# Differential outputs kept in SBUF, later preparations, and quadrant sums from a whole copy of transposed h

## The chip, the core and the metric

The kernel runs on one core of one Trainium2 chip. The metric is the device time of one execution in microseconds (us), as the median of several runs. Beside it stands one profiled execution, from which every view of the trace comes.

## What is computed

Two layers of a decoder trunk over x of 1024 rows by 1024 channels in float32. Cut to what matters here:

```python
h = _rmsnorm(x, pre_g)
p = h @ w_in                       # q, k, v, gates, conv inputs, merge gates
y_fox  = _fox_attention(...)  * silu(fg)    # 8 heads of 64
o = _rmsnorm(a @ v, norm_g) * (1.0 - lam_init)   # differential attention, 4 heads of 128
y_diff = o * silu(dg)
y_conv = cb * _short_conv(cc * cx, conv_w) * silu(cg)
m = gates[0] * (y_fox @ w_fox) + gates[1] * (y_diff @ w_diff) + gates[2] * (y_conv @ w_conv)
x = x + _rmsnorm(m @ w_o, post_g)  # h of the next layer comes from this x
```

## The kernel before

**Numbers as pairs.** Every float32 operand of a matrix product is kept as two tiles, `hi` and `lo`: ScalarE (ACT) writes `hi`, a rounded copy, and VectorE (DVE) or GpSimd (POOL) writes `lo`, the rest (`split`, L373 and L374). One product is three matmuls (`mm3`, L352 to L354). Weights are loaded by SP into `wraw`, ACT makes `whi` (L277, L319) and POOL, or DVE, makes `wlo` (L280, L320).

**Head of a layer.** `norm_rows` normalises rows (`hn`, L402) and TensorE (PE) transposes them into PSUM tiles `T` of 128x512, of which there are two (L175). From each `T` come one `hi` and one `lo` piece of `ht`. So h stands transposed in 16 blocks: two halves of the rows, four pairs of channel groups, hi and lo. PE then runs a stretch of plain products of `ht` with the conv weights. Beside it `build_s` forms sums of h's quadrants (`s1` to `s4`, two sets j = 0 and 1) for Strassen products, seven in place of eight. A quadrant is hi plus lo, so the sum of two quadrants takes three adds on DVE (L445), and a set takes ten. Each sum is split into hi (ACT, L449) and lo (L451: DVE for s2 and s3, POOL for s1 and s4). The weights of the Strassen products need differences as well (`sw`, L322, on DVE) and are then split. DVE also runs the convolution (`cv`, L582 and L585) and gathers the products (`u` L564, `uv` L530).

**Tail of a layer.** Attention runs in eight windows, four fox, then four differential. A differential unit `g` of head `hd` ends in `squares` (ACT), a matmul with ones (PE, L1052), `norm` (ACT: Ln L1042, Exp L1043) and `out` (DVE, L1046), and ACT issues a DMA of the result to DRAM, `od` (L1048). `y_prep` for that head loads the whole head back, `o` (SP, L1098), and the gate `g` (SP, L1104), takes the sigmoid (ACT, L1114), multiplies (DVE, L1111) and splits the result into `y` (ACT L1116, POOL L1117). `merge_br` loads a weight `wraw<-wbr`, a merge gate `g<-mg` and `mf`, multiplies y by the weight (`T`, `F`, `S`, `O` are PSUM tiles) and gathers with L1143 and L1146. When the windows are over, PE has only these merges and the output projection.

**What sets the order.** Actions of `later(dt, fn)` are put on a heap with a due time on a model clock; the clock is moved by `tick` as main work is written, and `need(item)` runs the heap up to that item. The engines' orders are fixed when the program is built. An engine takes its instructions in that order; one that waits holds all behind it, and so does SP with its DMAs. `blk` tiles come from one pool of 41 blocks (`NBLK`) of 4 KB a partition; a tile for which no block is free waits for the last user of an old one.

Of the kernel before, what the change touches and what calls it, by code (L numbers as in the profile page):

```python
# [11 lines left out]
F32 = mybir.dt.float32  # L12
# [8 lines left out]
S = 1024  # L21
D = 1024
P = 128
# [112 lines left out]
class Trunk:  # L136
# [248 lines left out]
    def new_ht(self):  # L385
        return [[[self.blk([P, 2, 512], F32R, "ht") for _ in range(2)] for _ in range(4)] for _ in range(2)]

    def hk(self, h, k, o=0, n=512):

        return [t[:, k % 2, o:o + n] for t in self.hT[h][k // 2]]  # L390

    def norm_rows(self, xs, gB, hT, tb0, step):

        nc = self.nc
        ss = self.sm(4, "q")
        hs = [self.blk([P, D], F32, "hn") for _ in xs]
        for i0 in range(0, len(xs), step):
            for i in range(i0, i0 + step):
                nc.scalar.activation(hs[i], xs[i], AF.Square, accum_out=ss[:, i:i + 1])
            r = self.rstd(ss[:, i0:i0 + step], 1.0 / D)  # L400
            for i in range(i0, i0 + step):
                nc.vector.scalar_tensor_tensor(out=hs[i], in0=xs[i], scalar=r[:, i - i0:i - i0 + 1], in1=gB,  # L402
                                               op0=ALU.mult, op1=ALU.mult)
        for i in range(0, len(xs), 2):
            o = (tb0 + i) * P
            for kp in range(4):
                t = self.pT()
                for j in range(4):
                    k = 2 * kp + j // 2
                    self.transpose(t[:, j * P:(j + 1) * P], hs[i + j % 2][:, k * P:(k + 1) * P])  # L410
                hi, lo = (x[:, :, o:o + 256] for x in hT[kp])
                self.split(hi, lo, t.rearrange("p (k c) -> p k c", k=2))

# [21 lines left out]
    def build_s(self, L):  # L435
# [6 lines left out]
        for j in range(2):  # L442
            q = dict(a11=h0[j], a12=h0[j + 2], a21=h1[j], a22=h1[j + 2])
            f = {n: [t.rearrange("p k c -> p (k c)").bitcast(F32) for t in v] for n, v in q.items()}
            add = lambda o, a, b, op: nc.vector.tensor_tensor(out=o, in0=a, in1=b, op=op)  # L445
# [7 lines left out]

            g = {}
            for n, x, y, op in (("s1", "a21", "a22", ADD), ("s3", "a11", "a21", SUB)):
                t = g[n] = self.blk([P, 1024], F32, n)
                add(t, f[x][0], f[y][0], op)
                add(t, t, f[x][1], ADD)
                add(t, t, f[y][1], op)
                if n == "s1":  # L460
                    t2 = self.blk([P, 1024], F32, "s2")
                    add(t2, t, f["a11"][0], SUB)
                    add(t2, t2, f["a11"][1], SUB)
                    put("s2", t2)
                put(n, t)
            for x in range(2):
                nc.scalar.dma_start(L.a21[j, x], f["a21"][x])
            add(t2, f["a12"][0], t2, SUB)
            add(t2, t2, f["a12"][1], ADD)
            put("s4", t2)  # L470
            for n in ("a11", "a12", "a22"):
                L.a[n].append(q[n])

# [533 lines left out]
    def diff_unit(self, L, hd, g):  # L1007
# [14 lines left out]
        def stage2():  # L1022
# [10 lines left out]
            po = yield from self.pv_group(g, probs, vmm, W2D, 0.64)  # L1033
            t = self.tmp()
            o, r = t[:, :256], t[:, 256:512]

# [8 lines left out]
            def out():  # L1045
                nc.vector.scalar_tensor_tensor(out=o, in0=o, scalar=self.dgc[:, l:l + 1], in1=r,  # L1046
                                               op0=ALU.mult, op1=ALU.mult)
                nc.scalar.dma_start(L.o["d"][hd, :, g * 256:g * 256 + 256], o)  # L1048

# [3 lines left out]
            later(1.2, norm)  # L1053
            later(2.0, out)

# [38 lines left out]
    def y_prep(self, L, kind, c):  # L1094

        nc, later = self.nc, self.clock.later
        o, g = self.blk([P, S], F32, "o"), self.blk([P, S], F32, "g")
        nc.sync.dma_start(o, L.o[kind][c])  # L1098
        if kind == "f":
            rb = self.blk([P, S], F32, "rb")  # L1100
# [6 lines left out]
        for h in range(2):  # L1107
            o1, g1, hi, lo = (t[:, h * 512:h * 512 + 512] for t in (o, g, *y[:2]))
            if kind == "f":
                nc.gpsimd.tensor_tensor(out=o1, in0=o1, in1=rb[:, h * 512:h * 512 + 512], op=ALU.mult)  # L1110
            mul = lambda o1=o1, g1=g1: nc.vector.tensor_tensor(out=o1, in0=o1, in1=g1, op=ALU.mult)  # L1111
            later(0.0, mul)
            if raw:
                later(0.0, lambda g1=g1: nc.scalar.activation(g1, g1, AF.Sigmoid))  # L1114
                later(0.6, mul)
            later(1.0, lambda o1=o1, hi=hi: nc.scalar.copy(hi, o1))  # L1116
            y.append(later(1.6, lambda o1=o1, hi=hi, lo=lo: nc.gpsimd.tensor_tensor(  # L1117
                out=lo, in0=o1, in1=hi.bitcast(F32), op=ALU.subtract)))
# [82 lines left out]
    def layer(self, l):  # L1201
# [10 lines left out]
        L.g = {"fg": dt([4, P, S], "fg"), "dg": dt([4, P, S], "dg"), "mg": dt([16, P, S], "mg")}  # L1212
        L.o = {"f": dt([4, P, S], "of"), "d": dt([4, P, S], "od")}
        L.ff = self.smalls.tile([P, 8, 8], F32, tag="ff", name=self.nm("ff"), bufs=1)
# [21 lines left out]
        for pair in rest:  # L1236
            self.gates_spilled(L, *pair)
        self.run_behind()
        self.reload_a21(L)
        run(self.v_unit(L, "f", 1, self.bank))  # L1240
# [166 lines left out]
```

## Time and profile before

| | |
|---|---|
| median of three runs | 2555.74 us (2550.59 to 2557.41) |
| the profiled execution | 2551.78 us, of which the span in the trace is 2550.0 us |
| TensorE clock granted, mean | 0.983 of full |
| PE busy | 2424.3 us, 95% of the span |
| DVE, ACT, POOL busy | 1551.5, 1113.6, 807.2 us |
| chain that ended last | PE 75%, DVE 10%, POOL 4%, ACT 4%, issue 4%, DMA 3% |

[...] The four stretches that follow are the head and the tail of the two layers: about 20 to 125 us and 1270 to 1395 us, and about 1050 to 1140 us and 2317 to 2405 us.

### The profile page before, as it was taken

How to read it: one execution, taken by the hardware profiler on the slowest of the kernel's cores; microseconds unless marked ns; L12 is line 12 of the kernel's file. 1: busy time of each engine (PE TensorE's matmuls, PEld its weight loads, DVE VectorE, ACT ScalarE, POOL GpSimd, SP SyncE). 2: the span in 40 equal slices, each digit the busy share in tenths (PEclk: the TensorE clock that was granted, in tenths of full speed). 3: DMA queues.
4: the chain of work that ended last, by engine and by line, in shares of the span. 5: the costliest groups of instructions: out<-in, count | busy, mean ns of one | idle time of the engine just before them, and what ended most of it. 6: DMA issues, size and time to landing. Idle time of an engine off the chain costs nothing.

```text
span 2550.0 us, 35609 instructions
## 1 busy us (share of the span) xinstructions
PE 2424.3 (95%) x13112; PEld 2045.7 (80%) x13112; DVE 1551.5 (61%) x2809; ACT 1113.6 (44%) x2264; POOL 807.2 (32%) x565
## 2 busy tenths in 40 slices
PE   7899999999999999979997999999999999999898
PEld 6677887788889788758976778887889897887688
DVE  6966465645665665646578664356465646656554
ACT  4224333335565555454432242233365645445543
POOL 1566334431111112451035662355211111124500
PEclk9899999999999999989998999999999999999899
DMA  4012224542223335634521122344422223355434
GB/s 168 33 50 98 91 93 141 165 146 59 70 75 97 115 102 159 213 146 141 187 103 42 50 91 86 101 145 136 159 75 60 68 93 109 110 170 192 182 108 182
DMA packets 123709, 293.95 MB, mean 115 GB/s; under 512 B 16256, under 2 KB 41216, under 8 KB 123536
## 3 DMA queue, kind: packets, MB, share of 16 engines
q1 hardware_dynamic: 68720, 216.89, 24.8%
q10 hardware_dynamic: 54816, 74.79, 9.6%
q8 instruction: 104, 1.70, 0.3%
q14 instruction: 69, 0.57, 0.1%
HBM read 200.26 MB, written 72.48 MB: 107 GB/s over the span
## 4 chain that ended last, share of the span: by engine, by line
PE 75%; DVE 10%; POOL 4%; ACT 4%; issue 4%; DMA 3%; ACTq 0%; SPq 0%; POOLq 0%; DVEq 0%
PE F L352 11%; PE F L354 10%; PE F L353 10%; PE S L352 5%; PE S L354 5%; PE S L353 5%; PE T L175 4%; PE T L352 3%; PE T L354 3%; PE T L353 3%; PE S L836 3%; PE S L837 2%; DVE s L445 2%; POOL wlo L320 2%; PE O L354 2%
## 5 line engine op out<-in xcount | busy, mean ns | idle before, releaser
L280 POOL TENSOR_TENSOR wlo<-wraw,whi 128x1024 fp32r<-128x1024 f32 (+2 forms) x93 | 194.3, 2093 | 875.6 <-ACT whi L277 761.4
L352 PE MATMUL F<-ht,wlo 128*128 128x512 f32 x792 | 331.0, 418 | 0.0
L354 PE MATMUL F<-ht,whi 128*128 128x512 f32 x792 | 315.9, 399 | 0.0
L353 PE MATMUL F<-ht,whi 128*128 128x512 f32 x792 | 313.7, 396 | 0.0
L320 POOL TENSOR_TENSOR wlo<-sw,whi 128x512 fp32r<-128x512 f32 x160 | 229.0, 1442 | 216.3 <-ACT whi L319 190.6
L320 POOL TENSOR_TENSOR wlo<-wraw,whi 128x1024 fp32r<-128x1024 f32 x80 | 160.4, 2007 | 168.3 <-ACT whi L319 158.7
L319 ACT CAST whi<-sw 128x512 fp32r<-128x512 f32 x160 | 96.0, 619 | 246.1 <-DVE sw L322 106.5
L354 PEld LDWEIGHTS F<-ht,whi 128*128 128x128 f32 x792 | 149.5, 189 | 32.4
L875 DVE TENSOR_TENSOR pt<-T,pt 128x512 fp32r<-128x512 f32 (+1 forms) x240 | 147.9, 633 | 43.6 <-ACT pt L874 41.1
L352 PEld LDWEIGHTS F<-ht,wlo 128*128 128x128 f32 x792 | 151.0, 191 | 24.4 <-ACT ht L373 0.4
L353 PEld LDWEIGHTS F<-ht,whi 128*128 128x128 f32 x792 | 150.7, 190 | 24.0
L988 ACT ACTIVATE p<-S,sm 128x512 f32<-128x512 f32 (+2 forms) x192 | 110.5, 580 | 132.7 <-DVE sm L984 61.4
L277 ACT CAST whi<-wraw 128x1024 fp32r<-128x1024 f32 (+2 forms) x126 | 117.8, 939 | 91.6 <-PE F L354 26.9
L982 DVE TENSOR_REDUCE sm<-S 128x1 f32<-128x512 f32 (+2 forms) x192 | 103.0, 553 | 79.5 <-PE S L840 50.6
L874 ACT CAST pt<-T 128x512 fp32r<-128x512 f32 (+1 forms) x240 | 124.5, 544 | 57.5 <-PE T L175 37.8
L836 PE MATMUL S<-qk,qk 128*128 128x512 f32 (+2 forms) x384 | 138.8, 361 | 6.5 <-ACT p L988 6.3
L175 PE MATMUL T<-ident,p 128*128 128x128 f32 x864 | 128.8, 274 | 2.0 <-DVE pt L875 0.9
L837 PE MATMUL S<-qk,sw 128*128 128x512 f32 (+2 forms) x384 | 129.3, 342 | 0.0
L908 ACT ACTIVATE p<-p,sm 128x384 f32<-128x384 f32 (+7 forms) x128 | 99.5, 777 | 62.6 <-DVE sm L901 54.3
L319 ACT CAST whi<-wraw 128x1024 fp32r<-128x1024 f32 x80 | 66.7, 834 | 137.6 <-PE S L354 40.6
L352 PE MATMUL F<-whi,ht 128*128 128x256 f32 (+1 forms) x416 | 122.8, 295 | 0.0
L354 PE MATMUL F<-whi,ht 128*128 128x256 f32 (+1 forms) x416 | 117.5, 282 | 0.0
(376 smaller groups left out, 6993.8 us busy)
## 6 DMA issues: line engine op xcount, KB each, us to landing
wraw<-wt SPq DMA_DIRECT2D x128, 512.0 KB
mg<-tmp ACTq DMA_DIRECT2D x64, 256.0 KB
sw<-qk ACTq DMA_DIRECT2D x256, 64.0 KB
g<-mg SPq DMA_DIRECT2D x32, 512.0 KB
wraw<-wo SPq DMA_DIRECT2D x32, 512.0 KB
x<-x SPq DMA_DIRECT2D x24, 512.0 KB
wraw<-wbr SPq DMA_DIRECT2D x48, 256.0 KB
m<-tmp ACTq DMA_DIRECT2D x32, 256.0 KB
```

Of the source, the lines that this page charges most:

```text
L175: self.nc.tensor.transpose(out, x, self.ident)
L277: nc.scalar.copy(hi, raw)
L280: getattr(nc, eng).tensor_tensor(out=lo, in0=raw, in1=hi.bitcast(F32), op=ALU.subtract)
L319: nc.scalar.copy(w[0][:, o], f)
L320: nc.gpsimd.tensor_tensor(out=w[1][:, o], in0=f, in1=w[0][:, o].bitcast(F32), op=ALU.subtract)
L352: nc.tensor.matmul(ps, wl, xh, start=start and i == 0, stop=False)
L353: nc.tensor.matmul(ps, wh, xl, start=False, stop=False)
L354: nc.tensor.matmul(ps, wh, xh, start=False, stop=stop and i == n - 1)
L836: nc.tensor.matmul(ps[:, :wp], q[:, i * P:(i + 1) * P], k[:, c0:c0 + wp], start=True, stop=False)
L837: nc.tensor.matmul(ps[:, :wp], qsw[:, (i % 2) * P:(i % 2) * P + P], k[:, c0:c0 + wp], start=False, stop=not last)
L874: self.clock.later(0.1, lambda: nc.scalar.copy(hi, T[:, n0:]))
L875: done = self.clock.later(0.6, lambda: nc.vector.tensor_tensor(out=lo, in0=T[:, n0:], in1=hi.bitcast(F32), op=ALU.subtract))
```

## The change

Three parts.

**A whole copy of transposed h.** `new_ht` makes three tiles for each place: hi, lo, and a float32 tile with the whole value. `norm_rows` fills the third with a copy on ACT from the same PSUM tile `T`. `build_s` reads only the third, so one add makes a sum of two quadrants. A layer has 16 such copies (128x512) more and its L445 adds go from 20 to 8. The 24 blocks are held until the gates are through; then `self.hT` keeps hi and lo alone.

**Differential outputs in SBUF.** A head's output gets a block `od` at its first unit; the units write into it, and `y_prep` waits for the last one (`od_done`) and works in it. The DMAs of L1048 (16 a layer, 128 KB) and the loads of L1098 for these heads (4 a layer, 512 KB) are gone.

**Later due times.** In `y_prep` the steps move from 0.0, 0.0, 0.6, 1.0, 1.6 to 4.0, 4.0, 4.6, 5.0, 5.6, and the fox heads' multiplication on POOL, until now at once, is asked for at 3.0.

```diff
     def new_ht(self):
-        return [[[self.blk([P, 2, 512], F32R, "ht") for _ in range(2)] for _ in range(4)] for _ in range(2)]
+        return [[[self.blk([P, 2, 512], dt, "ht") for dt in (F32R, F32R, F32)] for _ in range(4)] for _ in range(2)]
...
-                hi, lo = (x[:, :, o:o + 256] for x in hT[kp])
-                self.split(hi, lo, t.rearrange("p (k c) -> p k c", k=2))
+                hi, lo, f = (x[:, :, o:o + 256] for x in hT[kp])
+                tv = t.rearrange("p (k c) -> p k c", k=2)
+                self.split(hi, lo, tv)
+                nc.scalar.copy(f, tv)
...
-            f = {n: [t.rearrange("p k c -> p (k c)").bitcast(F32) for t in v] for n, v in q.items()}
+            f = {n: v[2].rearrange("p k c -> p (k c)") for n, v in q.items()}
...
-            for n, x, y, op in (("s1", "a21", "a22", ADD), ("s3", "a11", "a21", SUB)):
-                t = g[n] = self.blk([P, 1024], F32, n)
-                add(t, f[x][0], f[y][0], op)
-                add(t, t, f[x][1], ADD)
-                add(t, t, f[y][1], op)
...
-            add(t2, f["a12"][0], t2, SUB)
-            add(t2, t2, f["a12"][1], ADD)
+            t1, t2, t3 = (self.blk([P, 1024], F32, n) for n in ("s1", "s2", "s3"))
+            add(t1, f["a21"], f["a22"], ADD)
+            add(t2, t1, f["a11"], SUB)
+            put("s2", t2)
+            put("s1", t1)
+            add(t3, f["a11"], f["a21"], SUB)
+            put("s3", t3)
...
+            add(t2, f["a12"], t2, SUB)
             put("s4", t2)
...
-            t = self.tmp()
-            o, r = t[:, :256], t[:, 256:512]
+            r = self.tmp((P, 256))
+            if g == G_ORDER[0]:
+                L.od[hd] = self.blk([P, S], F32, "od")
+            o = L.od[hd][:, g * 256:g * 256 + 256]
...
-                nc.scalar.dma_start(L.o["d"][hd, :, g * 256:g * 256 + 256], o)
...
-            later(2.0, out)
+            end = later(2.0, out)
+            if g == G_ORDER[-1]:
+                L.od_done[hd] = end
...
-        nc.sync.dma_start(o, L.o[kind][c])
-        if kind == "f":
+        if kind == "d":
+            while c not in L.od_done:
+                yield 0.0
+            self.clock.need(L.od_done[c])
+            o = L.od[c]
+        else:
+            o = self.blk([P, S], F32, "o")
+            nc.sync.dma_start(o, L.o[kind][c])
...
-            later(0.0, mul)
+            later(4.0, mul)
...
-            later(1.0, lambda o1=o1, hi=hi: nc.scalar.copy(hi, o1))
-            y.append(later(1.6, lambda o1=o1, hi=hi, lo=lo: nc.gpsimd.tensor_tensor(
+            later(5.0, lambda o1=o1, hi=hi: nc.scalar.copy(hi, o1))
+            y.append(later(5.6, lambda o1=o1, hi=hi, lo=lo: nc.gpsimd.tensor_tensor(
```

The change moves instructions at three places. Line numbers of the kernel after are two to six lines off those of before: L414 is the new copy, L447 the add (L445 before), L453 the lo (L451), L451 the hi (L449), L578 and L581 the convolution (L582, L585), L560 the gathering (L564), L1109 the load of the gate (L1104).

DVE in the head of the second layer, second set of sums, before. `s3_2082` is the last sum that takes three adds, `sw` of the row with a single `wraw` is the weight difference of the product with s3:

```order
L451 TENSOR_TENSOR s_2079_12126<-s_2077_12122,s_2078_12125 128x1024
L445 TENSOR_TENSOR s_2082_12133<-ht_10686,ht_10694 128x1024
L445 TENSOR_TENSOR s_2077_12122<-ht_10690,s_2077_12122 128x1024
L445 TENSOR_TENSOR s_2082_12133<-s_2082_12133,ht_10687 128x1024
L445 TENSOR_TENSOR s_2077_12122<-s_2077_12122,ht_10691 128x1024
L322 TENSOR_TENSOR sw_11920<-wraw_11901 128x512
L445 TENSOR_TENSOR s_2082_12133<-s_2082_12133,ht_10695 128x1024
L564 TENSOR_TENSOR u_11885<-u_11885,O_12175 128x512
```

The same place after (`s_2094` is s3, `sw_11934` the difference, `u_11899<-u_11899,O_12177` the gathering of the last plain product):

```order
L447 TENSOR_TENSOR s_2094_12128<-ht_10680,ht_10692 128x1024
L447 TENSOR_TENSOR s_2093_12127<-ht_10686,s_2093_12127 128x1024
L560 TENSOR_TENSOR u_11898<-u_11898,S_12075 128x512
L453 TENSOR_TENSOR s_2100_12141<-s_2094_12128,s_2099_12140 128x1024
L322 TENSOR_TENSOR sw_11923<-wraw_11914,sw_11923 128x512
L578 TENSOR_SCALAR cv_11900<-u_11898,par 128x1024
L581 SCALAR_TENSOR_TENSOR cv_11900<-u_11898,par,cv_11900 128x1023
L581 SCALAR_TENSOR_TENSOR cv_11900<-u_11898,par,cv_11900 128x1022
L560 TENSOR_TENSOR u_11899<-u_11899,T_12151 128x512
L560 TENSOR_TENSOR u_11899<-u_11899,O_12177 128x512
L578 TENSOR_SCALAR cv_11901<-u_11899,par 128x1024
L322 TENSOR_TENSOR sw_11934<-wraw_11915 128x512
```

Four adds stood ahead of the difference and one behind it; now all sums are done before the plain products end, and one step of the convolution stands right ahead of the difference.

ACT in the same head, the last four tiles `T`, before (`a<-ht` are DMAs of a quadrant to DRAM):

```order
L373 CAST ht_10692<-T_11844 128x2x256
L467 DMA a_11883<-ht_10692 128x1024
L373 CAST ht_10694<-T_11851 128x2x256
L373 CAST ht_10696<-T_11858 128x2x256
L467 DMA a_11883<-ht_10693 128x1024
L373 CAST ht_10698<-T_11865 128x2x256
```

And after, where each copy L414 waits for the lo (DVE) of the same tile, and the transposes of the next tile but one wait for the copy:

```order
L373 CAST ht_10687<-T_11855 128x2x256
L464 DMA a_11897<-ht_10687 128x1024
L414 COPY ht_10689<-T_11855 128x2x256
L373 CAST ht_10690<-T_11863 128x2x256
L464 DMA a_11897<-ht_10688 128x1024
L414 COPY ht_10692<-T_11863 128x2x256
L373 CAST ht_10693<-T_11871 128x2x256
L464 DMA a_11897<-ht_10690 128x1024
L414 COPY ht_10695<-T_11871 128x2x256
L373 CAST ht_10696<-T_11879 128x2x256
```

A copy now stands between one tile's hi and the next tile's.

SP in the tail of the first layer, the last two heads, before:

```order
L1098 DMA o_10165<-od_328 128x1024
L1104 DMA g_10166<-dg_325 128x1024
L1098 DMA o_10183<-od_328 128x1024
L1104 DMA g_10184<-dg_325 128x1024
L272 DMA wraw_10189<-wbr 128x512
L1128 DMA g_10195<-mg_326 128x1024
L1131 DMA mf_10197<-m_321 128x1024
```

And after:

```order
L1109 DMA g_10160<-dg_349 128x1024
L1109 DMA g_10176<-dg_349 128x1024
L272 DMA wraw_10180<-wbr 128x512
L1134 DMA g_10186<-mg_350 128x1024
L1137 DMA mf_10188<-m_345 128x1024
```

The load of the last head's output, which waited for the write of that output, no longer stands ahead of the gate and the weight.

## Rows read from the trace of the kernel before

**Rows 1.** PE's waits, 60 to 125 us: line, waited for, us in total, times, longest

```profile
PE S L352 <- ACT s L449: 5.1, 1, 5.1
PE F L352 <- ACT s L449: 4.1, 1, 4.1
...
PE F L353 <- DVE s L451: 1.2, 1, 1.2
```

**Rows 2.** PE's waits, 1300 to 1400 us

```profile
PE F L352 <- POOL wlo L320: 8.6, 1, 8.6
PE T L175 <- DVE hn L402: 4.4, 2, 2.8
PE T L352 <- POOL wlo L320: 4.0, 1, 4.0
PE S L352 <- POOL wlo L320: 1.0, 1, 1.0
```

**Rows 3.** PE's waits, 1085 to 1140 us

```profile
PE T L352 <- POOL wlo L280: 8.2, 1, 8.2
PE O L1029 <- ACT pt L874: 7.2, 2, 4.9
```

**Rows 4.** PE's waits, 2350 to 2405 us

```profile
PE F L352 <- POOL wlo L280: 9.2, 1, 9.2
PE O L1029 <- ACT pt L874: 2.7, 2, 2.3
PE S L352 <- POOL wlo L280: 1.7, 1, 1.7
```

**Rows 5.** Ten windows at half clock: us, busy (instructions) of PE, PEld, DVE, ACT, POOL, PEclk, DMA

```profile
1130.70:1137.60 6.90, 3.52 (x8) 2.82 (x9) 6.03 (x8) 4.36 (x8) 4.84 (x4) 0.51 1.03 408
...
1352.60:1362.80 10.20, 4.03 (x10) 3.17 (x11) 10.20 (x8) 3.62 (x5) 5.68 (x4) 0.50 0.00 1
...
sum 58.04, PE 37.50 PEld 30.15 DVE 44.59 ACT 23.46 POOL 33.17; mean PE 3.75 PEld 3.02 DVE 4.46 ACT 2.35 POOL 3.32
```

**Rows 6.** Lines L445, L373, L374 by form: ns min/median/max, first and last start

```profile
L445 DVE TENSOR_TENSOR s<-s,ht x28: 1209/1224/3424, 47.6 to 1356.4; 128x1024 f32<-128x1024 f32 x28
L445 DVE TENSOR_TENSOR s<-ht,ht x8: 1211/3423/3428, 41.9 to 1346.9; 128x1024 f32<-128x1024 f32 x8
...
L373 ACT CAST ht<-T x32: 578/587/602, 13.6 to 1311.0; 128x512 fp32r<-128x512 f32 x32
...
L374 DVE TENSOR_TENSOR ht<-T,ht x32: 675/691/693, 16.3 to 1311.6; 128x512 fp32r<-128x512 f32 x32
```

**Rows 7.** The chain of waits that ended last, 1340 to 1360 us, by line

```profile
by line: DVE s L445 63.0%; DVE sw L322 12.2%; DVE s L451 11.8%; issue 7.4%; ACT s L449 5.3%; DVE u L564 3.0%; DVEq L451 0.1%
```

**Rows 8.** Timeline, 1354 to 1360 us: start us, us, engine, line, instruction

```profile
1352.44 3.41 DVE L445 TENSOR_TENSOR s<-s,ht 128x1024 f32<-128x1024 f32 x2
1355.78 0.68 DVE L322 TENSOR_TENSOR sw<-wraw 128x512 f32<-128x512 f32 x1
...
1357.18 1.54 POOL L320 TENSOR_TENSOR wlo<-sw,whi 128x512 fp32r<-128x512 f32 x1 [3.55 <-ACT whi L319]
```

**Rows 9.** Timeline of SP, ACT and POOL, 1122 to 1134 us

```profile
1124.95 0.32 SPq L1098 DMA_DIRECT2D o<-od  x1
...
1123.15 0.33 ACTq L1048 DMA_DIRECT2D od<-tmp  x1
1130.26 1.28 ACT L1114 ACT_TABLE_LOAD   x1 [6.62 <-DMA g<-dg]
...
1132.76 1.26 POOL L280 TENSOR_TENSOR wlo<-wraw,whi 128x512 fp32r<-128x512 f32 x1 [6.98 <-ACT whi L277]
```

**Rows 10.** Timeline of ACT, 1095.5 to 1102.5 us

```profile
1095.92 1.28 ACT L1114 ACT_TABLE_LOAD   x1
...
1101.58 0.96 ACT L874 CAST pt<-T 128x512 fp32r<-128x512 f32 x2
```

**Rows 11.** Timeline of DVE, 1299 to 1306.5 us

```profile
1300.23 4.57 DVE L402 SCALAR_TENSOR_TENSOR hn<-x,y,gB 128x1024 f32<-128x1024 f32 x2
```

More of the change, by code (lines that the diff above doesn't have):

```diff
@@ L385, in new_ht @@
     def new_ht(self):
-        return [[[self.blk([P, 2, 512], F32R, "ht") for _ in range(2)] for _ in range(4)] for _ in range(2)]
+        return [[[self.blk([P, 2, 512], dt, "ht") for dt in (F32R, F32R, F32)] for _ in range(4)] for _ in range(2)]
     def hk(self, h, k, o=0, n=512):
-        return [t[:, k % 2, o:o + n] for t in self.hT[h][k // 2]]
+        return [t[:, k % 2, o:o + n] for t in self.hT[h][k // 2][:2]]
     def norm_rows(self, xs, gB, hT, tb0, step):
@@ L452, in put @@
                 L.a[n].append([t.rearrange("p (k c) -> p k c", k=2) for t in (hi, lo)])
-            g = {}
-            for n, x, y, op in (("s1", "a21", "a22", ADD), ("s3", "a11", "a21", SUB)):
-                t = g[n] = self.blk([P, 1024], F32, n)
-                add(t, f[x][0], f[y][0], op)
-                add(t, t, f[x][1], ADD)
-                add(t, t, f[y][1], op)
[L460 to L467, printed above, removed]
-            add(t2, f["a12"][0], t2, SUB)
-            add(t2, t2, f["a12"][1], ADD)
+            t1, t2, t3 = (self.blk([P, 1024], F32, n) for n in ("s1", "s2", "s3"))
[5 more added lines that the diff above has]
+            put("s3", t3)
+            for x, t in enumerate(q["a21"][:2]):
+                nc.scalar.dma_start(L.a21[j, x], t.rearrange("p k c -> p (k c)").bitcast(F32))
+            add(t2, f["a12"], t2, SUB)
             put("s4", t2)
             for n in ("a11", "a12", "a22"):
-                L.a[n].append(q[n])
+                L.a[n].append(q[n][:2])
     def reload_a21(self, L):
@@ L1096, in y_prep @@
         nc, later = self.nc, self.clock.later
-        o, g = self.blk([P, S], F32, "o"), self.blk([P, S], F32, "g")
-        nc.sync.dma_start(o, L.o[kind][c])
-        if kind == "f":
+        g = self.blk([P, S], F32, "g")
+        if kind == "d":
[6 more added lines that the diff above has]
+            nc.sync.dma_start(o, L.o[kind][c])
             rb = self.blk([P, S], F32, "rb")
@@ L1109, in y_prep @@
             if kind == "f":
-                nc.gpsimd.tensor_tensor(out=o1, in0=o1, in1=rb[:, h * 512:h * 512 + 512], op=ALU.mult)
+                later(3.0, lambda o1=o1, rb1=rb[:, h * 512:h * 512 + 512]: nc.gpsimd.tensor_tensor(
+                    out=o1, in0=o1, in1=rb1, op=ALU.mult))
             mul = lambda o1=o1, g1=g1: nc.vector.tensor_tensor(out=o1, in0=o1, in1=g1, op=ALU.mult)
-            later(0.0, mul)
+            later(4.0, mul)
             if raw:
-                later(0.0, lambda g1=g1: nc.scalar.activation(g1, g1, AF.Sigmoid))
-                later(0.6, mul)
-            later(1.0, lambda o1=o1, hi=hi: nc.scalar.copy(hi, o1))
-            y.append(later(1.6, lambda o1=o1, hi=hi, lo=lo: nc.gpsimd.tensor_tensor(
+                later(4.0, lambda g1=g1: nc.scalar.activation(g1, g1, AF.Sigmoid))
+                later(4.6, mul)
+            later(5.0, lambda o1=o1, hi=hi: nc.scalar.copy(hi, o1))
+            y.append(later(5.6, lambda o1=o1, hi=hi, lo=lo: nc.gpsimd.tensor_tensor(
                 out=lo, in0=o1, in1=hi.bitcast(F32), op=ALU.subtract)))
@@ L1212, in layer @@
         L.g = {"fg": dt([4, P, S], "fg"), "dg": dt([4, P, S], "dg"), "mg": dt([16, P, S], "mg")}
-        L.o = {"f": dt([4, P, S], "of"), "d": dt([4, P, S], "od")}
+        L.o = {"f": dt([4, P, S], "of")}
+        L.od, L.od_done = {}, {}
         L.ff = self.smalls.tile([P, 8, 8], F32, tag="ff", name=self.nm("ff"), bufs=1)
@@ L1238, in layer @@
         self.run_behind()
+        self.hT = [[t[:2] for t in half] for half in self.hT]
         self.reload_a21(L)
```

## The prediction

> **What bounds the kernel now.** I read the shares of busy time first: PE is busy for 95% of the span, so a gain has to come from the other 5% and from matmuls that run at the half clock. Then I read PE's waits, stretch by stretch. They gather in two places of each layer: the head, where the quadrant sums are made, and the tail, where attention has ended and the merges go on. In the first head PE waits for the sums themselves, 5.1 + 4.1 + 1.2 = 10.4 us [rows 1]. In the second head it waits 8.6 + 4.0 + 1.0 = 13.6 us for the low part of a weight [rows 2], but that is only the last link. The chain of waits over that stretch puts 63% on L445, the adds [rows 7], and the timeline says why: the difference `sw` that the weight is made of starts at 1355.78 us, behind adds of 3.41 us for two, and POOL's lo starts at 1357.18 and lasts 1.54 [rows 8]. So DVE bounds that stretch, not POOL. In the tails PE waits 8.2 and 7.2 us in the first layer [rows 3], and 9.2 + 2.7 + 1.7 = 13.6 us in the second [rows 4]. The 8.2 us end on the lo of a weight at 1132.76; before it ACT waited 6.62 us for the gate `g<-dg` [rows 9]. SP could ask for that gate only after `o<-od` at 1124.95, and that load waited for the write `od<-tmp` of 1123.15, so SP's line was shut by one transfer and opened too late for everything behind it [rows 9]. The 7.2 us wait for `pt` of ACT, which from 1095.92 did a table load and the steps of `y_prep` and reached the `pt` casts at 1101.58 [rows 10].
>
> After a wait the clock is at half: the granted clock reads 0.50 in ten stretches at these places, and PE worked 37.50 us in them [rows 5]. At most half of that, 18.75 us, is lost.
>
> **Part 1, adds away, copies added.** A layer loses 12 of 20 adds. One add took 1.22 us in the median where both inputs are sums or pieces, and 3.42 where two pieces of h are read [rows 6], so 12 x 1.22 = 15 to 12 x 3.42 = 41 us of DVE time. What of it counts is the wait that it caused, the 10.4 and the 13.6 us. Against it stands the copy on ACT. It is not in the trace; the nearest row is the hi of the same tile, 0.587 us [rows 6]. In the order of ACT it stands behind the tile's lo of 0.691 [rows 6], and the transposes of the next tile but one wait for it. A turn of a tile is then 0.59 + 0.69 + 0.59 = 1.87 us, and since ACT takes hi, copy, hi, copy, four tiles of a row pair need 4 x 1.87 = 7.5 us. Before, they needed between 4 x 0.59 + 0.69 = 3.1 and 4 x 1.28 = 5.1. So a row pair takes 2.4 to 4.4 us more; I take 3.4.
>
> Nothing in the trace shows ACT and DVE reading one PSUM tile together, so the turn of 1.87 rests on the order alone. [...]
>
> *First head.* All rows of x are there at the start, so little stands between the tiles: between one row pair's 3.4 and two pairs' 6.8 us I take 6, late for the plain products. With 12 adds fewer, s2 and s3 are ready before PE asks, so the 10.4 us go. Next late is the weight of the product with s3: its difference stands on DVE behind three steps of the convolution. The nearest rows for one such step are the 128x1024 adds, 1.2 to 3.4 us [rows 6], so 3.7 to 10 us, of which the products ahead hide about half: 4.5, with ends 0 and 8. Sum: -10.4 + 6 + 4.5 = +0.1; ends -7 and +6.
>
> *Second head.* Here the rows come from the output projection two at a time. The norm of the last pair (two `hn`, 4.57 us from 1300.23 [rows 11]) stands on DVE behind the third pair's lo pieces and so starts 3.4 later; with the last pair's own 3.4 that is up to 6.8. But PE's order now has whole products of the first half between these transposes, and the 4.4 us that PE waits for `hn` today [rows 2] stay about what they are; I take 2.5 as seen by PE, ends 0 and 6.8. The 13.6 us go: all sums are done before the plain products end, one step of the convolution (1.2 to 3.4) stands ahead of the difference, and three Strassen products ahead of its user. I leave 2.5 for what is late next, POOL's lo pieces in line, ends 0 and 6. Sum: -13.6 + 2.5 + 2.5 = -8.6; ends -13.6 and -0.8.
>
> **Parts 2 and 3, the tails.** They take away 16 writes a layer, 0.33 us of ACT each [rows 9], and four loads on SP. SP's line then holds, for the last head, the gate, the weight and the merge inputs, and none waits for the last unit's output any more: the gate waits only for a block that the first head's y frees. From SP's opening at 1124.95 to the gate's landing it took 5.3 us [rows 9], and this now passes beside attention. PE ran out of work at 1134.0 - 8.2 = 1125.8. Next late is ACT: after the last unit's norm, which is done by 1123.15 when its write is issued [rows 9], come the sigmoid's table of 1.28, some four activations and casts of 0.6 and the weight's hi among them, then POOL's 1.26: 1123.15 + 1.28 + 4 x 0.6 + 1.26 = 1128.1. It comes somewhat earlier since fewer table loads stand between the last norms, and somewhat later by waits on DVE between the steps: 1127 to 1129. So 2.5 of the 8.2 us stay in the first layer and 3 of the 9.2 in the second; ends 0 and 6. The waits for `pt` lie elsewhere: the steps of `y_prep` are asked for 4 us later, so ACT's order has the `pt` casts ahead of them and a merge product stands ahead of PE's last matmuls with `pt`. But the same sigmoid table load stays among the exponentials, so I keep half: 3.6 of 7.2, and 2.2 of 4.4. Sums: -(8.2 + 7.2) + 2.5 + 3.6 = -9.3, ends -15 and -3; and -13.6 + 3 + 2.2 = -8.4, ends -13 and -3.
>
> **Blocks.** The copies hold 8 more blocks of 41 in the head, the outputs up to 4 in the windows. I cost that at nothing, since the waits for blocks that I see in the order end on work that lies well back. If that cover is gone, one load comes late and costs what the gate cost, 5.3 us.
>
> **Clock.** Where a wait goes, its half-clock stretch goes with it. Of the 18.75 us I take back 10.5, about in the share of the waits that go; ends 3 and 16.
>
> **The sum.** 0.1 - 8.6 - 9.3 - 8.4 - 10.5 = -36.7 us against the profiled run of 2551.8: 2515.1. The median of the runs lies 4.0 above the profiled one; with the same distance the forecast is 2519 us.
>
> **Rivals.** *Only one place pays.* If the copies eat the heads' gain, the tails alone give 17.7 and half the clock, 5, so 2533 us; if ACT's table loads hold the tails as the gate did, the heads alone give 8.5 and 5, so 2542. For it speaks that ACT is in order and has to do both norm and sigmoid at the end; against it that the wait on the gate is 6.62 us of idle ACT, which is room.
>
> *Nothing to be measured.* Both happen: the heads give the copies what the adds gave up, and the tails save 3 each: 2549 to 2556. For it speaks that PE's two transposition tiles are the narrow point in the first head; against it that the chain over the second head is 63% adds.
>
> *Slower.* The copies in line with the tiles are seen in full: four row pairs a layer, two layers, 8 x 3.4 = 27 us, while the weights' low parts on POOL hold the products as before, so the heads give nothing; less the tails' 17.7 it is 2565 us. It decides if PE has no other work beside the transposes, in both heads. In the first pairs of a row half PE does have it, which speaks against. [...]
>
> *It doesn't do what it says.* The order shows the adds, writes and loads gone, so I give this nothing.
>
> **How the numbers follow.** The forecast (2503 to 2532) has 0.64, one place 0.22 (2532 to 2546), no change 0.08, slower 0.06. The range: the five terms have half-widths of 5 to 7 us, some 13 together if they are independent, so 2519 - 16 = 2503 below; above it takes in the rival of one place, 2546. What is left out is no change and slower, 0.14. About 0.3%, 8 us, can be told from no change, so faster is 0.64 + 0.22 = 0.86, same 0.08, slower 0.06.
>
> **What would show it.** In the head: L447 eight times a layer; PE's waits for ACT and DVE sums in the first head gone; the wait for L320 in the second under 3 us; against it longer waits of transposes for the copy and for `hn`. In the tail: SP asks for the last gate before 1115 us, the wait for L280 falls to 1 to 4 us, `pt` to about half. Fewer than ten half-clock stretches. The prediction is wrong if plain products end more than 7 us later than before in both heads, or if the tail's wait is back at 8 us under another name.

## The result and the profile after

The changed kernel takes 2523.82 us (median; 2521.85 to 2525.12), the kernel before, run beside it, 2556.39 (2550.59 to 2557.41). The ratio is 0.9877 with an interval of 0.9859 to 0.9894: faster by 32.6 us, where 2519 us (36.7 less) had been forecast, with a range of 2503 to 2546. The profiled execution of after took 2525.12 us, 1.3 above its median, whereas that of before lay 4.6 below its own; so the two spans are only 26.8 us apart.

The head of the page of after; PE had been busy 2424.3 us of a span of 2550.0:

```profile
span 2523.2 us, 35542 instructions
...
PE 2416.4 (96%) x13112; PEld 2040.0 (81%) x13112; DVE 1536.6 (61%) x2785; ACT 1126.8 (45%) x2294; POOL 809.5 (32%) x565
```

PE does the same 13112 matmuls. Its busy time fell by 7.9 us, which goes with the clock (below), and its idle time from 125.7 to 106.8, by 18.9. To see where, I cut each profiled execution at four points that all kernels have: the first matmul of attention (L704 before, L700 after) and the first of the output projection, in each layer. Lengths of the pieces in us, worked out from the start times of these matmuls; the last three columns anticipate the experiments below:

| piece | before | after | forecast of the difference, clock included | measured | copy first | third `sw` buffer | both |
|---|---|---|---|---|---|---|---|
| to first attention (first head) | 570.1 | 570.7 | -2.9 | +0.6 | 559.0 | 563.8 | 555.2 |
| attention and first tail | 615.8 | 603.2 | -11.5 | -12.6 | 603.6 | 602.9 | 600.7 |
| output projection, second head | 649.4 | 641.0 | -12.2 | -8.4 | 637.4 | 631.2 | 628.8 |
| attention and second tail | 613.8 | 607.5 | -10.1 | -6.3 | 605.4 | 603.6 | 602.7 |
| last output projection | 100.9 | 100.9 | 0 | 0 | 100.8 | 100.8 | 100.8 |

(The forecast is the prediction's four sums with the 10.5 us of the clock spread over them, 3.0, 2.2, 3.6 and 1.7 in the order of the table; this split is mine, the prediction gives only the whole.) Both tails and the second head gained; the first head gained nothing that these profiles can tell: four kernels with the same code in the first piece took 565.4 to 571.2 us for it (last section).

**First head.** PE's waits from 11.6 to 110 us in after (line, waited for, us in total, times, longest):

```profile
PE T L175 <- ACT ht L414: 8.5, 5, 3.4
PE S L352 <- POOL wlo L320: 8.2, 1, 8.2
...
PE O L352 <- ACT ht L373: 0.7, 1, 0.7
PE S L352 <- ACT ht L373: 0.7, 1, 0.7
```

The waits on the sums of [rows 1], 10.4 us, are gone. In their place stand 8.5 us in which transposes wait for the new copy, and 8.2 for the low part of one weight. In before, the transposes had waited 3.4 us at this place, for the lo pieces (11.6 to 60 us of before):

```profile
PE T L175 <- DVE ht L374: 3.4, 2, 2.9
```

**Second head.** PE's waits from 1265 to 1400 us in after; they answer to [rows 2]:

```profile
PE T L175 <- DVE hn L402: 10.5, 4, 6.5
PE F L352 <- POOL wlo L320: 3.7, 1, 3.7
```

The 13.6 us for weights became 3.7; the wait for `hn`, 6.3 us in before from 1270 to 1400, became 10.5.

**Tails.** PE's waits in the first tail (1040 to 1130 us), then in the second (2320 to 2405), against [rows 3] and [rows 4]:

```profile
PE O L1026 <- DVE pt L871: 3.1, 1, 3.1
PE S L832 <- ACT p L984: 2.3, 1, 2.3
PE F L352 <- POOL wlo L280: 1.6, 1, 1.6
PE O L1025 <- ACT pt L870: 1.6, 1, 1.6
...
PE T L352 <- POOL wlo L280: 0.6, 1, 0.6
```

```profile
PE S L352 <- POOL wlo L280: 1.7, 1, 1.7
PE T L352 <- POOL wlo L280: 1.6, 1, 1.6
PE O L1025 <- ACT pt L870: 1.6, 1, 1.6
...
PE F L352 <- POOL wlo L280: 1.1, 1, 1.1
PE O L1026 <- DVE pt L871: 1.0, 1, 1.0
```

The waits on L280 went from 8.2 to 2.2 and from 10.9 to 4.4. The timeline of SP shows the cause that the prediction named; the last gate, behind which the weight and the merge inputs stand, is now asked for at 1086.17 us, and it had been 1125.36, after the load of [rows 9]:

```profile
1086.17 0.32 SPq L1109 DMA_DIRECT2D g<-dg  x1
1086.54 0.42 SPq L272 DMA_DIRECT2D wraw<-wbr  x1
```

**Clock.** The windows at half clock that answer to those of [rows 5] (columns as there):

```profile
43.30:50.20 6.90, 5.25 (x14) 3.84 (x15) 1.68 (x3) 2.73 (x5) 0.00 (x0) 0.51 0.40 156
94.50:104.80 10.30, 5.31 (x13) 4.15 (x14) 10.18 (x10) 1.62 (x3) 4.87 (x4) 0.50 0.16 51
...
1289.20:1302.90 13.70, 6.92 (x21) 5.27 (x22) 8.45 (x8) 6.67 (x13) 2.71 (x1) 0.50 0.49 191
...
sum 47.90, PE 33.54 PEld 26.14 DVE 35.84 ACT 17.47 POOL 18.76; mean PE 4.79 PEld 3.73 DVE 5.12 ACT 2.50 POOL 2.68
```

Seven windows with 33.54 us of PE, where [rows 5] has ten with 37.50. But [rows 5] is not all: in the same heads and tails of before the clock also read 0.50 from 117.0 to 120.4, from 1277.5 to 1280.9 and from 2318.6 to 2322.0 us, with 3.40 us of PE in each. So it is thirteen windows with 47.7 us against seven with 33.5. I estimate that half of the 14.2 us between them, 7.1, is what the half clock no longer costs there, which is most of the 7.9: in after, matmuls of 128x512 follow one another by 0.43 us from 1054 to 1057 us, where the clock reads 0.50, and by 0.23 from 1171.8 to 1173.9, where it reads 1.00. Three of the seven are new: in before the clock read 1.00 from 43.3 to 50.2 and from 1289.2 to 1302.9 us, and 0.83 from 94.5 to 104.8. They stand behind the copies of the first head, about the late weight, and about the longer `hn`.

### The profile page after: what moved, and what is told of

Read it like the earlier page. It is cut to its first block, busy times and chain, and to the rows that moved or that the text cites. A ratio compares the mean times of both kernels' runs of the same rounds, so it can differ in the third digit from the quotient of the medians.

```text
span 2523.2 us, 35542 instructions
## 1 busy us (share of the span) xinstructions
PE 2416.4 (96%) x13112; PEld 2040.0 (81%) x13112; DVE 1536.6 (61%) x2785; ACT 1126.8 (45%) x2294; POOL 809.5 (32%) x565
## 4 chain that ended last, share of the span: by engine, by line
PE 72%; DVE 11%; ACT 4%; POOL 4%; issue 4%; DMA 3%; ACTq 1%; SPq 0%; POOLq 0%; DVEq 0%
PE F L352 10%; PE F L354 10%; PE F L353 10%; PE S L352 5%; PE S L354 5%; PE S L353 5%; PE T L175 4%; PE T L352 3%; PE T L354 3%; PE T L353 3%; PE S L832 2%; PE S L833 2%; POOL wlo L320 2%; PE O L352 2%; PE O L354 2%
## 5 line engine op out<-in xcount | busy, mean ns | idle before, releaser
L280 POOL TENSOR_TENSOR wlo<-wraw,whi 128x1024 fp32r<-128x1024 f32 (+2 forms) x93 | 195.9, 2109 | 866.3 <-ACT whi L277 738.1
L320 POOL TENSOR_TENSOR wlo<-sw,whi 128x512 fp32r<-128x512 f32 x160 | 226.5, 1426 | 217.9 <-ACT whi L319 192.2
L320 POOL TENSOR_TENSOR wlo<-wraw,whi 128x1024 fp32r<-128x1024 f32 x80 | 158.4, 1982 | 173.5 <-ACT whi L319 167.0
L352 PE MATMUL F<-whi,ht 128*128 128x256 f32 (+1 forms) x416 | 122.8, 295 | 0.0
L322 DVE TENSOR_TENSOR sw<-wraw,sw 128x512 f32<-128x512 f32 x80 | 77.8, 972 | 71.7 <-POOL wlo L320 70.8
```

Source lines behind the costliest of these rows:

```text
L280: getattr(nc, eng).tensor_tensor(out=lo, in0=raw, in1=hi.bitcast(F32), op=ALU.subtract)
L320: nc.gpsimd.tensor_tensor(out=w[1][:, o], in0=f, in1=w[0][:, o].bitcast(F32), op=ALU.subtract)
L352: nc.tensor.matmul(ps, wl, xh, start=start and i == 0, stop=False)
```

## Experiments

### The parts alone

Three theories stood. Mine: heads and tails gain separately, by the adds and by SP's line. A rival: one place alone pays. Another: the due times, not the outputs in SBUF, make the tails' gain.

**Part 1 alone**: the changes in `new_ht`, `norm_rows` and `build_s`, the tails as before.

```
+                nc.scalar.copy(f, tv)
...
+            f = {n: v[2].rearrange("p k c -> p (k c)") for n, v in q.items()}
```

> Part 1 alone: the whole copy of transposed h and the shorter quadrant sums; outputs through DRAM and due times as before. My theory (heads and tails are independent, and the copy in line with the tiles costs the first head what the adds gave): the first head comes out 2 to 4 us later than before, the second 6 to 8 us earlier, the tails unchanged with 8 to 9 us of waiting for a weight's lo from L280; about 2548 us against 2556, 2544 to 2552. The rival (the sums are what matters, and the tails' gain is a by-product of them): 2530 or less. The other rival (the copies cost more than they give): 2558 or more.

Measured: 2546.94 us against 2558.73 of before, ratio 0.9957 (0.994 to 0.9973). The head's pieces are 569.8 and 640.5 us, so -0.3 and -8.9 against before; PE's waits in both heads are those of after to a tenth or two (8.5 and 8.2; the `wlo` of the second head 3.7). The time is where I had put it; the first head, though, did not come out 2 to 4 us later.

**Parts 2 and 3 alone**, the heads as before:

```
+                L.od[hd] = self.blk([P, S], F32, "od")
...
-            later(0.0, mul)
+            later(4.0, mul)
```

> Parts 2 and 3 alone: differential outputs in SBUF and later due times; sums as before. My theory: both tails gain as in the changed kernel, 12 and 6 us in the trace, and the heads stay: 2535 us, 2530 to 2540; waits for L280 in the tails under 3 us, the waits for the sums in the first head 10 us as before. The rival (tails gain only part, the rest comes from the heads): 2545 or more.

Measured: 2532.29 us, ratio 0.9896 (0.9876 to 0.9917). Its first head waits as in [rows 1], its first tail as that of after; the time is as expected.

11.8 us for part 1 and 26.4 for the rest make 38 against 32.6 together; by the intervals, some 4 to 5 us wide on each side, that cannot be told from the sum. The heads and the tails gain separately.

**Part 2 alone**, with the due times of before:

```
-                nc.scalar.dma_start(L.o["d"][hd, :, g * 256:g * 256 + 256], o)
...
+            self.clock.need(L.od_done[c])
+            o = L.od[c]
```

> Part 2 alone: differential outputs in SBUF, due times of the preparations as before. My theory (the line of SP, shut by the load of an output that was still being written, made the long wait of the tails): the waits of 8.2 and 9.2 us for L280 fall under 3 us, the waits for the casts of pt stay at about 7 and 3 us or grow; 2542 us, 2537 to 2547. The rival (the due times do the work): within 4 us of before, 2552 to 2560.

**Part 3 alone**, the outputs still by way of DRAM:

```
-            later(0.0, mul)
+            later(4.0, mul)
```

> Part 3 alone: later due times of the preparations, outputs through DRAM. My theory: the waits for the casts of pt fall by half, but the load of the last output still shuts SP's line and the long wait for L280 stays at 8 us or grows, since the steps after it are asked for later; 2550 us, 2545 to 2560. The rival (the due times do the work of parts 2 and 3): 2535 to 2540.

Part 2 alone measured 2528.56 us, ratio 0.9889 (0.9864 to 0.9913); part 3 alone 2546.27, ratio 0.9955 (0.9937 to 0.9973). The first lies below the 2537 to 2547 that I expected, so the outputs in SBUF do more than I thought: they make all of the tails' gain that can be measured, and the due times add nothing beside them, though alone they are worth some 12 us. PE's waits in the first tail, of part 2 alone (1075 to 1130 us) and then of part 3 alone (1085 to 1140):

```profile
PE O L1029 <- ACT pt L874: 4.4, 2, 4.1
PE T L352 <- POOL wlo L280: 2.4, 1, 2.4
```

```profile
PE T L352 <- POOL wlo L280: 4.8, 1, 4.8
PE O L1030 <- DVE pt L875: 2.9, 1, 2.9
PE O L1029 <- ACT pt L874: 2.8, 2, 1.7
```

I had put the whole of the `pt` gain on the due times. In fact 7.2 us fell to 4.4 without them, and with them the wait for L874 fell to 2.8 but 2.9 for L875 on DVE came up. And I had thought that SP's line would stay shut in part 3 alone. Its timeline of ACT shows why it opened earlier:

```profile
1116.50 1.28 ACT L1042 ACT_TABLE_LOAD   x1 [0.94 <-DVE tmp L1046]
...
1118.28 1.28 ACT L1043 ACT_TABLE_LOAD   x1
...
1120.55 0.33 ACTq L1048 DMA_DIRECT2D od<-tmp  x1
1121.18 1.28 ACT L1115 ACT_TABLE_LOAD   x1 [1.19 <-DVE o L1112]
```

The last unit's Ln (L1042) and Exp (L1043) now stand together, ahead of the sigmoid. In before, a sigmoid with its table stood between them (1118.94 to 1120.87 us), so the write went out at 1123.15; here it goes at 1120.55. SP's load `o<-od` still waits for it, but goes out 2.6 us earlier. Both parts shorten the same line, which would explain why they do not add; no run shows it by itself.

### What the copy costs

In the first head the transposes wait for the copy. Either the copy costs because ACT has one instruction more, or because it holds the PSUM tile behind the hi and the lo. To tell these apart: the same copy, but first, with hi and lo made from the copy in SBUF. ACT does the same work; the tile is free after one step.

```
                 tv = t.rearrange("p (k c) -> p k c", k=2)
-                self.split(hi, lo, tv)
                 nc.scalar.copy(f, tv)
+                self.split(hi, lo, f)
```

> The changed kernel with the whole copy taken first, and hi and lo formed from that copy in SBUF, so that a transposition tile in PSUM is free after one step of 0.59 us in place of three. My theory (the time that a tile is held in PSUM makes the first head late): PE's waits for L414, 8.5 us in the first head, go, the plain products end 6 to 10 us earlier there and 2 to 4 us earlier in the second head; 2516 us against 2524 of the changed kernel, 2510 to 2520. The rival (ACT's own 16 copies a layer make it late, wherever they read from): the waits pass to hi, 2522 to 2527.

Measured: 2509.23 us, ratio 0.9822 (0.9806 to 0.9838), 14.6 us below after and just below what I expected, and the heads 11.7 and 3.6 us shorter (table). PE's waits in the first head (11.6 to 110 us) and ACT's timeline there:

```profile
PE S L352 <- POOL wlo L320: 4.8, 1, 4.8
PE T L175 <- ACT ht L413: 2.7, 4, 0.8
```

```profile
15.87 0.59 ACT L413 COPY ht<-T 128x512 f32<-128x512 f32 x1
16.49 0.62 ACT L373 CAST ht<-ht 128x512 fp32r<-128x512 f32 x1
17.02 0.58 ACT L413 COPY ht<-T 128x512 f32<-128x512 f32 x1
```

The wait for the copy falls from 8.5 to 2.7 us with as many instructions on ACT, and no wait stands between them any more. The wait for the weight's lo falls with it, from 8.2 to 4.8.

The other way: no copy at all; POOL makes the whole value from hi and lo in SBUF.

```
                 self.split(hi, lo, tv)
-                nc.scalar.copy(f, tv)
+                nc.gpsimd.tensor_tensor(out=f, in0=hi.bitcast(F32), in1=lo.bitcast(F32), op=ALU.add)
```

> The changed kernel with the whole copy formed on POOL, which has nothing to do at that time in the first head, as hi plus lo from SBUF, in place of the ACT copy from PSUM. My theory (the copy in line with the tile in PSUM is the cost, not the block or the shorter sums): PE's waits in the transposes are those of before (3.4 us for L374), the plain products end 5 to 10 us earlier in the first head; 2518 us, 2511 to 2523. The rival (POOL's adds hold up DVE's adds of two pieces in SBUF, which took 3.4 us beside POOL in place of 1.2): 2526 or more.

Measured: 2510.99 us, ratio 0.9828 (0.9813 to 0.9843), as good. Its transposes wait 6.7 us for the lo, where I had expected the 3.4 of before, and none for a copy. Together the two say that the time the PSUM tile is held was the price, not ACT's 0.59 us: the first keeps ACT's work and gains, the second takes it away and gains no more.

### What the weight's low part waits for

The 8.2 us for `wlo` in the first head end on POOL, but the chain behind it is DVE. The timeline of DVE in after, with the POOL instruction that PE waited for:

```profile
88.56 2.88 DVE L578 TENSOR_SCALAR cv<-u,par 128x1024 f32<-128x1024 f32 x1
91.48 4.36 DVE L581 SCALAR_TENSOR_TENSOR cv<-u,par,cv 128x1023 f32<-128x1023 f32 x2
...
96.36 0.68 DVE L322 TENSOR_TENSOR sw<-wraw 128x512 f32<-128x512 f32 x1
```

```profile
90.86 3.91 POOL L320 TENSOR_TENSOR wlo<-sw,whi 128x512 fp32r<-128x512 f32 x2
97.77 1.66 POOL L320 TENSOR_TENSOR wlo<-sw,whi 128x512 fp32r<-128x512 f32 x1 [3.01 <-ACT whi L319]
```

The difference `sw` stands behind three steps of the convolution, 7.24 us, as the prediction had read from the order. Why does it stand there? It needs a tile of the pool `swaps`, which has two, and one comes free only when POOL has made the lo of an earlier difference. POOL made two of these from 90.86 to 94.77 us, the first of them until 92.56; so even with no convolution ahead the difference could have started at most 3.8 us earlier. A third tile tells whether the place in line or the engine's work is the cause:

```
-            tc.tile_pool(name="swaps", bufs=2) as swaps,
+            tc.tile_pool(name="swaps", bufs=3) as swaps,
```

> The changed kernel with three buffers for the weight differences in place of two, so that the last difference need not wait until POOL has split the first. My theory (the difference comes late because of its buffer, and behind it the lo of the weight): the wait for L320 ahead of the product with s3 falls from 8.2 us to 3 or less in the first head and from 3.7 to 1.5 or less in the second; 2515 us, 2509 to 2520. The rival (POOL's line sets it, the difference is not late): 2522 to 2527, with the wait as before.

Measured: 2504.0 us, ratio 0.98 (0.9785 to 0.9814), 19.8 below after and 5 below the range that I expected. The difference is now made 55 us earlier, between lo pieces (timeline of DVE):

```profile
41.60 0.68 DVE L322 TENSOR_TENSOR sw<-wraw 128x512 f32<-128x512 f32 x1
```

In the second head no wait for L320 is left at all, and that piece is 9.8 us shorter than in after; the first head is 6.9 shorter, though 4.9 us of wait for another weight's `wlo` came up there. So the place in line, which the tile sets, was the cause of that wait, and not the adds or the convolution as such.

That raised a doubt about my reading of before: [rows 7] put 63% of the chain on the adds. If the third tile frees before as well, the adds were never the bound.

**Before with the third tile**, and **parts 2 and 3 with the third tile**:

> The kernel before with three buffers for the weight differences; nothing of the change. Two readings of the 8.6 us wait in its second head. The prediction's: the adds stand ahead of the difference on DVE and fill it; then with the difference early the sums themselves are late at the same place, 5 us or more of waiting stay in the second head and 10 us in the first; 2543 to 2550 us, by the smaller waits for L320 alone. The rival (the buffer alone made that wait, and the adds are hidden): the second head's wait falls under 3 us; 2530 to 2538.

> Parts 2 and 3 with three buffers for the differences, without part 1. Its distance to 2504 us (the changed kernel with three buffers) is what part 1 is worth when the differences are early. My theory (the sums of three adds bound both heads as soon as nothing else does, and the copies cost the first head about what they give): 2510 to 2520. The rival (with early differences part 1 is worth nothing, or costs): 2498 to 2506.

Measured: 2530.08 us, ratio 0.9886 (0.9862 to 0.9911), and 2511.01, ratio 0.9812 (0.9794 to 0.9829). PE's waits of before with the third tile, 1300 to 1400 us:

```profile
PE F L352 <- ACT s L449: 8.3, 1, 8.3
PE S L352 <- POOL wlo L320: 1.4, 1, 1.4
```

The two readings of the first of these runs part: its time lies in the rival's range, its waits are mine. In that stretch the reading holds: the long wait stays at 8.3 us where it was 8.6, and only its last link changes from the weight to the sum. The sums were as late as the weight. In the first head the waits for the sums stay as well, 5.8 + 4.7 + 1.1 us. But the buffer alone gains before 28.6 us: its pieces up to attention are 563.1 and 639.7 us, 7 and 9.7 shorter. The two profiles are 19.3 us apart; of that, eleven waits on L320 of 1.0 to 4.0 us, 23.1 in all, which I had passed over, became seven with 8.6, and the rest is not traced to lines. With the third tile, part 1 is worth 2511.01 - 2504.0 = 7 us in the medians and 3 by the ratios, whose intervals overlap; with copy first it is worth more, as 2490.09 against 2511.01 shows:

### Together

Copy first and the third tile, and the same with the due times of before (4.0, 4.0, 4.6, 5.0, 5.6 back to 0.0, 0.0, 0.6, 1.0, 1.6, and the POOL multiplication at once):

> Both: the copy first, and three buffers for the differences. My theory (two separate waits in a row): the gains add, 2507 us, 2500 to 2514. The rival (an earlier end of the plain products only moves PE's wait to the weights' lo, since DVE and POOL then set the head): 2514 to 2520.

> Copy first and three buffers, with the due times of before: what part 3 is worth beside the rest. My theory, from part 2 alone (2528.6) against parts 2 and 3 (2532.3): nothing that can be told; 2485 to 2495 against 2490. The rival (the due times are needed once the heads are short): 2498 or more.

Measured: 2490.09 us (2488.78 to 2492.39), ratio 0.9747 (0.9732 to 0.9762), and 2493.95, ratio 0.9745 (0.973 to 0.9761). The first beats both kernels, after by 33.7 us; the two gains, 14.6 and 19.8, add, where I had expected 2500 to 2514. The due times again make no difference that can be measured. Of all waits in the second head (1240 to 1380 us) one line is left:

```profile
PE T L175 <- DVE hn L402: 8.8, 3, 5.6
```

## Why the prediction was right, and where its steps were off

The forecast was right in its sign, its size (2519 against 2523.8) and in its main case: not one place pays, but both. That the size came so close is in part luck: the two profiled executions are only 26.8 us apart where the sum, built on rows of the one before, had 36.7, and several terms below are off one against another. Its steps, each with what came of it:

**The tails: right, but for the account of `pt`.** Of the first, -9.3 us in waits and 2.2 by the clock had been worked out, -12.6 came. The wait on the weight's lo was to stay at 2.5 us, and 2.2 stayed; SP asked for the gate at 1086, well before 1115. Of the 7.2 us for `pt` 3.6 were to stay; 4.7 did, 1.6 for ACT and 3.1 for DVE. In the second tail the prediction took 4.4 us for waits on `pt`, but 1.7 of these are for L280 [rows 4]; 4.4 us for L280 and 2.6 for `pt` are left there, where 3 and 2.2 had been forecast. This tail gave -6.3 in this execution; the six other profiled kernels with the same code for the tail gave -8.4 to -11.7, around the forecast of -10.1, so this one execution gained less there than the code is worth (last section). The step that failed is the account: the whole `pt` gain was given to the due times, and part 2 alone shows that the first 2.8 of 7.2 us go without them and that nothing measurable is lost by leaving them out.

**The turn of a tile: right, its effect too small.** The prediction put 1.87 us on hi, lo, copy. The timeline of ACT in the second head of after:

```profile
1282.38 0.59 ACT L414 COPY ht<-T 128x512 f32<-128x512 f32 x1 [0.76 <-DVE ht L374]
1282.87 0.59 ACT L373 CAST ht<-T 128x512 fp32r<-128x512 f32 x1
1284.22 0.59 ACT L414 COPY ht<-T 128x512 f32<-128x512 f32 x1 [0.76 <-DVE ht L374]
```

From copy to copy it is 1.84 us, and each copy waits 0.76 us for the lo. Copy and lo of one tile never ran together: each of the 32 copies of this profile began 0.03 us or more after the end of its tile's lo. With the copy beside the lo a turn would be 0.59 + 0.69 = 1.28 us, by an estimate from [rows 6]; the copy waits for the lo, so no run tries that. But the plain products ended later by more than 6 and 2.5 us: the matmul behind the last of them started at 82.77 us instead of 71.46 in the first head, 11.3 later, and 5.1 later in the second, counted from the first output projection. In the first head 6.5 us of it are waits in rows (8.5 + 0.7 + 0.7 against 3.4), and the 5.25 us at half clock behind them [43.3 to 50.2 above] cost up to 2.6 more; the rest I have no row for. With copy first it starts at 75.97. In waits the term is 6.5 against 6; as lateness of the products, which is how it was worked out, it was mis-sized: 11.3 against 6, beyond what I had allowed (6.8). The prediction's sign of being wrong, more than 7 us in both heads, came in one.

**The weight in the first head: right place, past the upper end, and part of the cause.** 4.5 us had been taken of 0 to 8, and 8.2 came. The step that failed is the price: the prediction gave the delay to the three steps of the convolution alone, and had about half of them hidden. They took 7.24 us, inside its 3.7 to 10, but their share of the wait is at most 3.8, since the tile of `swaps` came free at 92.56 at the earliest; the rest is the wait for that tile, which it had not counted. Then -10.4 + 6.5 + 8.2 is a loss of some 4 in waits where I had +0.1. The piece shows +0.6 because waits on L320 further on in it, 2.0 us at 117 and 3.6 at 406 in before among them, came to 4.3 us less; nothing in the prediction had counted on that.

**The second head: size off, sign right.** 13.6 us of weight waits were to leave 2.5 and left 3.7. "The 4.4 us that PE waits for `hn` stay about what they are" failed: 6.3 became 10.5, 4.2 more where 2.5 had been taken, with ends of 0 and 6.8. DVE's timeline shows it as the prediction had described it: the four lo pieces of the third row pair now start at 1281.66, 1283.49, 1285.32 and 1287.16 us, each behind a copy on ACT, and the norm's first step can follow only at 1287.76, 6.1 us behind the first lo. In before they were two and two without such gaps, and that step came 3.35 us behind. That is 2.75 us later (forecast 3.4), and the wait on `hn` shows it. Then -13.6 + 4.2 + 3.7 is -5.7 in waits against -8.6. Part 1's -8.9 and after's -8.4 in this piece stand against -12.2.

**The adds: right in number, wrong in what sets their price.** L447 stands at 8 a layer, and two pieces of h still take 3.42 us in the median (by form: ns min/median/max); but not because they are pieces of h, as the last section shows:

```profile
L447 DVE TENSOR_TENSOR s<-ht,ht x8: 1216/3420/3434, 55.9 to 1326.4; 128x1024 f32<-128x1024 f32 x8
...
L414 ACT COPY ht<-T x32: 577/587/613, 17.0 to 1306.8; 128x512 f32<-128x512 f32 x32
```

The copy took 0.587 us in the median, what its nearest row had given.

**The clock: 10.5 forecast, 7.9 measured** as PE's busy time, and nearer than the working deserved. Old half-clock stretches went with their waits, but three new ones came with the new waits, so that thirteen became seven; the forecast had counted only those that go. Against the ten that it had counted, only half of 37.50 - 33.54, or 2.0 us, is won by the same estimate; the three of before that it had missed make up most of the rest.

**Blocks: right in cost.** No wait of PE for a block showed in the heads or the tails. SP stood 17 us at a load of x in the second head (L1195, until 1269.58), which it had not in before, but DVE waited for ACT alone from 1260 to 1300 us, and not for x.

**What the prediction did not see.** It read the adds as the bound of the second head, which the run of before with a third tile bears out for that one stretch. It did not ask why the weight's difference stands where it does. The pool of two `swaps` sets that place, and its third buffer is worth 28.6 us to before: nearly as much as the whole change, in good part from small waits of 1 to 4 us that I had not grouped. And it did not ask why one add takes 1.2 us and the next 3.4.

Open stays how much of the 11.3 us in the first head is order and how much waiting, and what the same change with a fourth tile of `swaps` would do; neither was tried.

## What to carry to other kernels

When several results are made of one PSUM tile, copy it once to SBUF and make the rest from the copy: the tile is then held for one step and not for a chain over two engines (here the wait of the transposes fell from 8.5 to 2.7 us, and the time by 14.6). When an instruction stands late in an engine's order, ask which buffer it had to wait for before you blame the work ahead of it, and add up the small waits on one line over the whole program. And when two changes shorten the same line of waits (here the load behind a write, and the norm between two sigmoids), do not add what each gains alone. Before you price an instruction of DVE by its median, look at what POOL was doing when it began (here an add of 128x1024 took 1.71 to 3.43 us beside POOL and 1.21 to 1.23 without).

## What the runs showed of the hardware

In these profiles the time of one shape of one instruction goes with POOL. The adds of 128x1024 that read h (L445, L447) number 56 in before and after together. 24 of them began while POOL was at an instruction, and each took 1.71 to 3.43 us; 32 began with POOL idle, and each took 1.21 to 1.23. Two adds of two pieces of h in before, and two in after, are among the quick ones, so the pieces are not what makes an add slow. Lines of after, from the timelines of DVE and POOL:

```profile
82.34 3.43 DVE L447 TENSOR_TENSOR s<-ht,ht 128x1024 f32<-128x1024 f32 x1
85.69 1.21 DVE L447 TENSOR_TENSOR s<-ht,s 128x1024 f32<-128x1024 f32 x1
...
96.97 0.74 DVE L578 TENSOR_SCALAR cv<-u,par 128x1024 f32<-128x1024 f32 x1
```

```profile
81.57 3.12 POOL L453 TENSOR_TENSOR s<-s,s 128x1024 fp32r<-128x1024 f32 x1 [1.01 <-POOL wlo L320]
88.19 2.70 POOL L453 TENSOR_TENSOR s<-s,s 128x1024 fp32r<-128x1024 f32 x1 [3.50 <-ACT s L451]
```

The step of the convolution that took 2.88 us at 88.56 began beside POOL's instruction of 88.19; the one of 0.74 at 96.97 began while POOL was idle, from 94.77 to 97.77. No run moved POOL's work away from these adds, so what the change would gain by that stays open.

One profile does not fix the time of a stretch. The second attention and tail, of the same code, took 602.1 to 607.5 us in the profiles of seven kernels that differ elsewhere. The windows of that piece in after and in parts 2 and 3 alone (columns as in [rows 5]):

```profile
1814.90:2422.40 607.50, 591.26 (x3441) 500.18 (x3442) 388.70 (x910) 328.54 (x742) 146.35 (x127) 0.99 0.36 113
```

```profile
1818.30:2421.70 603.40, 589.19 (x3441) 499.33 (x3442) 388.70 (x910) 328.82 (x742) 146.62 (x127) 0.99 0.36 114
```

The same 3441 matmuls kept PE busy 2.07 us longer in the one than in the other, half of the 4.1 us between them. In after the clock read 0.50 over 9.26 us of PE's work (from 1814.9 and 2343.9 us), which by the estimate above cost up to 4.6; its mean is 0.99 in both, and how much of the difference is the clock's is not shown. The first piece differs as much. Before, parts 2 and 3 together, part 2 and part 3 have the same instructions there, in the same order on every engine, and took 570.1, 565.4, 566.2 and 571.2 us. So one profile tells such a stretch to some 5 us and no better.
